# Attention outputs of a decoder trunk: two matmuls with high and low values side by side in place of three, and one PSUM bank for each key head

## Chip, core and metric

The kernel runs on one core of one Trainium2 chip. The metric is the device time of one execution in microseconds (us); lower is better. Five engines run side by side: TensorE (PE, matmuls; PEld are its weight loads), VectorE (DVE), ScalarE (ACT), GpSimd (POOL), and SyncE (SP), which here issues the DMAs. Each engine takes its instructions strictly in the order in which the program lists them.

## The reference

Two layers, each of five blocks on a residual stream of 256 tokens by 1024 features: a gated feed-forward block, a mixer, a second feed-forward block and a per-layer input. The mixer has two branches. The change is in branch B, attention with a window of 128 keys, 16 query heads and 4 key heads (four query heads share a key head), 64 features per head:

```python
u = rmsnorm(h, mix_norm); z = u @ w_in
# B: 128-query blocks; each sees its own and the block before
scores = einsum("bnqhgd,bnkhd->bnhgqk", qb, kw) * 64 ** -0.5
pr = exp(where(valid, scores, -inf) - mx)
attn = pr / (sum(pr) + exp(sink - mx))
out = einsum("bnhgqk,bnkhd->bnqhgd", attn, vw)          # the attention outputs
merged = sigmoid(g_m) * (hm @ w_branch_m) + sigmoid(g_a) * (out @ w_branch_a)
h = h + merged @ w_out
```

Branch A is a recurrent one (mLSTM) with a short causal convolution on its queries and keys. Weights and activations are fp32.

## The kernel before, in words

Every fp32 matrix is kept as two fp32r tiles, a high part (ScalarE casts it) and a low part (VectorE subtracts the high part from the source); `splitting` at L464 does this. A product takes three matmuls, high by high, high by low and low by high (`mm3`, L386). The first name behind the arrow in a row is the moving operand of the matmul, the second the stationary one; for weights `wh` and `wl` are the two parts.

Weights stream from HBM in 1 MB pieces (tile `raw`) and are split into `wh` and `wl`; a ring of eight pairs feeds the matmuls. All matmul outputs go into one pool of eight PSUM banks, 128 by 512 fp32 each (`bank`, L246). A tile takes a bank that another has given back, and its first matmul then waits for the last reader of the tile that had the bank before.

The order of the work on PE, ACT, DVE and SP is written by the kernel itself. Jobs (the matmuls of a projection) run one after the other. Chains, which are generators such as `scores` and `outputs` below, are advanced one step at each `tick` (L196), as soon as a planner (`Clock`, L60 to 111, with a cost per element for each engine) thinks that their last step is done. The planner knows engines and DMAs; it holds no banks. What it decides becomes the fixed order of each engine's queue; at run time only semaphores hold an engine.

The mixer's jobs in order, with the tile names that the rows carry: `kvq` (keys, values, queries), `v` (mLSTM values), `gt` (gate), `if` (mLSTM gates), `z` twice (convolution inputs), `ya` (the attention outputs times `w_branch_a`, L790 to 798), `og`, `z`, `gt`, `ym`, `yo`. The attention chains run beside `kvq` to `ya`. For a block of queries t, a pair of key heads p and a key head g in it, `outputs` (L1220) scales the probabilities `pr`, transposes them on PE into a bank `tp`, splits that into `ptd`, and multiplies by the values. A key head has 64 features, so the values stand in `vpad` with zeros in the other 64 columns of the stationary tile: two key heads add into the two halves of one bank `ha`, three matmuls of 512 columns for each block s of keys. When both heads are in, `ha` is split into `haT`, which shares its tile with `qT` (rows show it as `qT<-ha`). Block t = 0 has one block of keys, t = 1 has two.

Other tiles in the rows: `wif` are the weights of the mLSTM gates, split by two small ACT and two small DVE instructions; `cv`, `cy`, `qk` belong to the convolution (`conv`, L991), whose VectorE steps read the bank `z`; `wt` and `w` are mLSTM decay weights; `xn` and `uT` the normalized residual stream and its transpose. L130 is the line that issues every recorded instruction, so rows are told apart by tiles.

Of the kernel before, what the change touches and what calls it, by code (L numbers as in the profile page):

```python
# [11 lines left out]
F32 = mybir.dt.float32  # L12
F32R = mybir.dt.float32r
BF16 = mybir.dt.bfloat16
AF = mybir.ActivationFunctionType
ALU = mybir.AluOpType
# [6 lines left out]
NT = T // P  # L23
# [3 lines left out]
NB = 512  # L27
# [3 lines left out]
AQ, AKV, AD = 16, 4, 64  # L31
# [18 lines left out]
class Part:  # L50


    def __init__(self, c0, k, n):
        self.c0, self.k, self.n = c0, k, n
        self.hi = self.lo = self.ready = None
        self.fresh = True
        self.rows = None


class Clock:  # L60
# [18 lines left out]
    def begin(self, **ready):  # L79
        outer = self.stage  # L80
        self.stage = {**(outer or {}), **ready}
        return outer
# [1012 lines left out]
class Swa:  # L1095

    def __init__(self, tr, l):
        self.tr, self.nc = tr, tr.nc  # L1100
        self.l = l
        self.haT = self.qT = tr.new_T("qT")
        self.vpad, self.inputs = {}, {}

    def prepare(self):
        tr, nc, a, l = self.tr, self.nc, self.tr.a, self.l
# [2 lines left out]

    def begin(self):  # L1110
        tr, nc = self.tr, self.nc
        for s in range(NT):
            v = tr.slot("vpad", F32R)[:, : 2 * NB].rearrange("p (x h d) -> p x h d", x=2, h=AKV)
            nc.gpsimd.memset(v.bitcast(F32), 0.0)
            for part in range(2):
                self.vpad[s, part] = v[:, part]
        self.kT = tr.slot("kT", F32R)[:, : 4 * T].rearrange("p (x b t) -> p x b t", x=2, b=2)
        self.nsink = tr.small.tile([P, AQ], F32, tag="nsink", bufs=2, name=tr.name("nsink"))
        nc.vector.tensor_scalar(self.nsink, self.sink, -1.0, None, op0=ALU.mult)
# [20 lines left out]
    def keys(self, t, ps):  # L1140
        tr, nc = self.tr, self.nc
        n = AKV * AD
        r = yield from self.rms(ps[:, :n], AKV)
        kn = tr.scr("kn")[:, :n]
        nc.vector.tensor_tensor(kn.rearrange("p (h d) -> p h d", d=AD), ps[:, :n].rearrange("p (h d) -> p h d", d=AD),
                                r[:, :, None].to_broadcast([P, AKV, AD]), op=ALU.mult)
        for g in range(2):
            v = ps[:, n:].rearrange("p (b g d) -> p b g d", g=2, d=AD)[:, :, g, :]
            o = [self.vpad[t, part].rearrange("p (b g) d -> p b g d", g=2)[:, :, g, g * AD : (g + 1) * AD]
                 for part in range(2)]  # L1150
            yield from tr.splitting(o[0], o[1], v)
        tok = slice(t * P, (t + 1) * P)
        yield
        yield from self.put(self.kT[:, 0, :, tok], self.kT[:, 1, :, tok], tr.transposes(kn, 2), tr.gk)
# [65 lines left out]
    def outputs(self, t, p, g, acc, hd, pr, mx, den):  # L1220

        tr, nc = self.tr, self.nc
        tok = slice(t * P, (t + 1) * P)
        es = tr.col("es", 4)
        nc.vector.tensor_tensor(es, mx, self.sink[:, hd], op=ALU.add)
        yield
        nc.scalar.activation(es, es, AF.Exp)
        yield
        nc.vector.tensor_tensor(den, den, es, op=ALU.add)
        nc.vector.reciprocal(den, den)  # L1230
        yield
        for j in range(4):
            nc.scalar.mul(pr[:, j, :], pr[:, j, :], den[:, j : j + 1])
        yield
        total = 2 * (t + 1)
        for s in range(t + 1):
            ps = tr.bank("tp")
            for j in range(4):
                nc.tensor.transpose(ps[:, j * P : (j + 1) * P], pr[:, j, s * P : (s + 1) * P], tr.ident)
            yield  # L1240
            ptd = tr.slot("ptd", F32R)[:, : 2 * NB].rearrange("p (x n) -> p x n", x=2)
            yield from tr.splitting(ptd[:, 0], ptd[:, 1], ps)
            yield
            if (t, p) not in acc:
                acc[t, p] = [tr.bank("ha"), 0]
            out, n = acc[t, p]
            acc[t, p][1] += 1
            tr.mm3(out, self.vpad[s, 0][:, 2 * p + g, :], self.vpad[s, 1][:, 2 * p + g, :], ptd[:, 0], ptd[:, 1],
                   n == 0, n == total - 1)
        if n == total - 1:  # L1250
            yield
            yield from tr.splitting(self.haT[0](4 * p, tok, 4), self.haT[1](4 * p, tok, 4),
                                    out.rearrange("p (j t) -> p j t", j=4))


@with_exitstack
# [25 lines left out]
```

## Time and profile before

| what | value |
|---|---|
| median of three runs | 1375.36 us (1374.87 to 1376.43) |
| the profiled execution | 1374.73 us, of which the span of instructions is 1372.9 us |
| PE busy, PEld busy | 99% and 90% of the span |
| DVE busy, ACT busy | 63% and 54% |
| mean granted TensorE clock | 1.000 |
| HBM read | 241.34 MB, 177 GB/s |

A busy share is the time in which an engine had at least one instruction in hand. Matmuls are pipelined: a row of one matmul lasts longer than the distance to the next matmul's start, so what a matmul costs is read from starts, not from durations. ACT and DVE overlap the end of an instruction with the start of the next in the same way by some 0.1 us. The three runs differ by 0.11%.

### The profile page before, as it was taken

The page shows a single profiled execution, that of the slowest core. Times are in us where ns is not written, and L with a number is a line of the kernel's source. Part 1 is how long each engine was busy: PE and PEld are TensorE (multiplying, and loading weights), DVE is VectorE, ACT ScalarE, POOL GpSimd, SP SyncE. Part 2 cuts the span into 40 slices and gives each one's busy share as a digit, 9 for nine tenths or more (in the row PEclk, how much of TensorE's full clock was granted, in tenths as well). Part 3 has the DMA queues.
Part 4 walks back from the last instruction along what each step waited for, and adds up shares of the span by engine and source line. Part 5 has one row for each costly group of instructions (what it writes and reads, how often), then busy time and mean ns, then how long its engine had stood idle before and what let it go on. Part 6 is the DMA issues. An engine that isn't in the chain of part 4 may idle for free.

```text
span 1372.9 us, 21950 instructions
## 1 busy us (share of the span) xinstructions
PE 1359.6 (99%) x9016; PEld 1231.6 (90%) x9016; DVE 867.7 (63%) x1332; ACT 738.7 (54%) x1148; POOL 58.3 (4%) x84
## 2 busy tenths in 40 slices
PE   8999999999999999999999999999999999999998
PEld 6999888899899899988879998878998998999886
DVE  5655558777786665554665554586877876655544
ACT  5554345887565444443555443468875654544433
POOL 0000012000000000000000000120000000000000
PEclk9999999999999999999999999999999999999999
DMA  6665646254645465565456566454546554755651
GB/s 207 223 209 174 224 131 215 95 168 114 224 155 196 156 216 189 167 234 184 162 161 215 171 200 215 149 165 140 144 113 228 185 179 155 227 186 175 210 182 62
DMA packets 125831, 243.82 MB, mean 178 GB/s; under 512 B 14977, under 2 KB 23841, under 8 KB 125730
## 3 DMA queue, kind: packets, MB, share of 16 engines
q1 hardware_dynamic: 125730, 242.41, 55.1%
q8 instruction: 71, 1.16, 0.3%
q14 instruction: 30, 0.25, 0.1%
HBM read 241.34 MB, written 1.05 MB: 177 GB/s over the span
## 4 chain that ended last, share of the span: by engine, by line
PE 91%; DMA 3%; DVE 3%; ACT 1%; issue 0%; POOL 0%; SPq 0%; ACTq 0%; POOLq 0%
PE dn L130 17%; PE pg L130 16%; PE pu L130 14%; PE gt L130 7%; PE z L130 7%; PE gu L130 6%; PE v L130 3%; PE ya L130 3%; PE ym L130 3%; PE og L130 3%; PE yo L130 3%; PE kvq L130 3%; PE tp L130 2%; DVE wl L130 1%; DMA raw<-in_ffn_w_gate_dram 1%; DMA raw<-in_w_in_dram 1%
## 5 line engine op out<-in xcount | busy, mean ns | idle before, releaser
L130 DVE TENSOR_TENSOR wl<-raw,wh 128x1024 fp32r<-128x1024 f32 (+1 forms) x448 | 539.7, 1222 | 338.8 <-ACT wh L130 338.0
L130 ACT CAST wh<-raw 128x1024 fp32r<-128x1024 f32 x448 | 459.8, 1049 | 392.1 <-PE dn L130 78.6
L130 PE MATMUL dn<-wh,hid 128*128 128x512 f32 x688 | 218.1, 395 | 0.0
L130 PE MATMUL pg<-uT,wh 128*128 128x256 f32 x1088 | 194.6, 281 | 0.0
L130 PE MATMUL pu<-uT,wh 128*128 128x256 f32 x1088 | 193.7, 280 | 0.0
L130 PEld LDWEIGHTS pg<-uT,wh 128*128 128x128 f32 x1088 | 166.9, 188 | 0.2
L130 PEld LDWEIGHTS pu<-uT,wh 128*128 128x128 f32 x1088 | 166.9, 188 | 0.0
L130 PEld LDWEIGHTS dn<-wh,hid 128*128 128x128 f32 x688 | 129.2, 188 | 30.0
L130 PE MATMUL pu<-uT,wl 128*128 128x256 f32 x544 | 153.1, 281 | 0.0
L130 PE MATMUL pg<-uT,wl 128*128 128x256 f32 x544 | 153.0, 281 | 0.0
L130 PE MATMUL dn<-wl,hid 128*128 128x512 f32 x352 | 138.8, 394 | 0.0
L130 PEld LDWEIGHTS pg<-uT,wl 128*128 128x128 f32 x544 | 102.5, 188 | 0.0
L130 PEld LDWEIGHTS pu<-uT,wl 128*128 128x128 f32 x544 | 102.4, 188 | 0.0
L130 PE MATMUL z<-uT,wh 128*128 128x256 f32 x512 | 93.0, 283 | 0.0
L130 PE MATMUL gt<-uT,wh 128*128 128x256 f32 x512 | 92.2, 282 | 0.0
L130 PE MATMUL gu<-wh,uT 128*128 128x512 f32 x256 | 84.1, 405 | 1.5 <-ACT uT L130 1.5
L130 PEld LDWEIGHTS dn<-wl,hid 128*128 128x128 f32 x352 | 66.2, 188 | 15.2
L130 PEld LDWEIGHTS gt<-uT,wh 128*128 128x128 f32 x512 | 78.9, 188 | 0.8
L130 PEld LDWEIGHTS z<-uT,wh 128*128 128x128 f32 x512 | 78.7, 188 | 0.4
L130 PE MATMUL z<-uT,wl 128*128 128x256 f32 x256 | 71.9, 281 | 0.0
L130 PE MATMUL gt<-uT,wl 128*128 128x256 f32 x256 | 71.9, 281 | 0.0
L130 PE MATMUL kvq<-wh,uT 128*128 128x512 f32 x192 | 63.7, 401 | 0.0
(192 smaller groups left out, 2040.8 us busy)
## 6 DMA issues: line engine op xcount, KB each, us to landing
raw<-in_w_in_dram SPq DMA_DIRECT2D x60, 1024.0 KB, 5.1
raw<-in_ffn_w_up_dram SPq DMA_DIRECT2D x40, 1024.0 KB, 5.1
raw<-in_ffn_w_down_dram SPq DMA_DIRECT2D x40, 1024.0 KB, 5.2
raw<-in_ffn_w_gate_dram SPq DMA_DIRECT2D x39, 1024.0 KB, 5.2
raw<-in_w_branch_a_dram SPq DMA_DIRECT2D x16, 512.0 KB, 6.0
raw<-in_w_branch_m_dram SPq DMA_DIRECT2D x8, 1024.0 KB, 6.4
raw<-in_w_out_dram SPq DMA_DIRECT2D x8, 1024.0 KB, 5.2
raw<-in_ple_gate_w_dram SPq DMA_DIRECT2D x8, 1024.0 KB, 6.9
```

Of the source, the lines that this page charges most:

```text
L130: return issue(*args, **kw)
```

## The change

The values of a key head are no longer padded. Their high and low parts stand side by side in the 128 columns of one stationary tile `vv`, the high part in the half where the head's outputs belong (columns 0 to 63 for g = 0, 64 to 127 for g = 1), the low part in the other. Two matmuls for each block of keys, with the high and the low part of `ptd` as moving operand, fill a bank of the head's own: one half holds the products with the high values, the other those with the low values. ScalarE copies the low half out of the bank into a scratch tile `hc` (64 partitions by 512), VectorE adds it to the high half. The first head's bank of a pair collects the result of both; the second head's VectorE instruction writes its sum into the other half of that bank. Then it is split as before. The two zeroing instructions on GpSimd for `vpad` are gone.

```diff
     def begin(self):
-        for s in range(NT):
-            v = tr.slot("vpad", F32R)[:, : 2 * NB].rearrange("p (x h d) -> p x h d", x=2, h=AKV)
-            nc.gpsimd.memset(v.bitcast(F32), 0.0)
-            for part in range(2):
-                self.vpad[s, part] = v[:, part]
+        v = tr.slot("vv", F32R)[:, : 2 * NB].rearrange("p (s h d) -> p s h d", s=NT, h=AKV)
+        self.vv = [v[:, s] for s in range(NT)]
...
-            o = [self.vpad[t, part].rearrange("p (b g) d -> p b g d", g=2)[:, :, g, g * AD : (g + 1) * AD]
-                 for part in range(2)]
+            o = [self.vv[t].rearrange("p (b g) d -> p b g d", g=2)[:, :, g, r * AD : (r + 1) * AD] for r in (g, 1 - g)]
...
-        total = 2 * (t + 1)
         for s in range(t + 1):
...
-            if (t, p) not in acc:
-                acc[t, p] = [tr.bank("ha"), 0]
-            out, n = acc[t, p]
-            acc[t, p][1] += 1
-            tr.mm3(out, self.vpad[s, 0][:, 2 * p + g, :], self.vpad[s, 1][:, 2 * p + g, :], ptd[:, 0], ptd[:, 1],
-                   n == 0, n == total - 1)
-        if n == total - 1:
+            if s == 0:
+                out = tr.bank("ha")
+            for x in range(2):
+                nc.tensor.matmul(out, self.vv[s][:, 2 * p + g, :], ptd[:, x], start=s + x == 0, stop=s == t and x == 1)
+        yield
+        rows = [slice(r * AD, (r + 1) * AD) for r in (g, 1 - g)]
+        rest = tr.scr("hc")[rows[0]]
+        nc.scalar.copy(rest, out[rows[1]])
+        yield
+        first = (t, p) not in acc
+        both = acc.setdefault((t, p), out)
+        nc.vector.tensor_tensor(both[rows[0]], out[rows[0]], rest, op=ALU.add)
+        if not first:
             yield
             yield from tr.splitting(self.haT[0](4 * p, tok, 4), self.haT[1](4 * p, tok, 4),
-                                    out.rearrange("p (j t) -> p j t", j=4))
+                                    both.rearrange("p (j t) -> p j t", j=4))
```

The planner sees other costs, so the queues change in the mixers of both layers, in the same way in each.

VectorE in layer 1, where the attention outputs of block t = 0, heads p = 0, come up, before:

```order
L130 TENSOR_TENSOR ptd_2585<-tp_2574,ptd_2585 128x512 [waits Activation_49]
L130 TENSOR_TENSOR ptd_2599<-tp_2587,ptd_2599 128x512 [waits Activation_49]
L130 TENSOR_TENSOR wl_2631<-raw_2464,wh_2630 128x1024 [waits Activation_49]
L130 TENSOR_TENSOR v_2510<-v_2535,v_2507 128x2x256 [waits Activation_49]
L130 TENSOR_TENSOR wif_2704<-wif_1576,wif_2704 128x8x4 [waits Activation_49] x2
```

and at the same place now:

```order
L130 TENSOR_TENSOR ptd_2596<-tp_2584,ptd_2596 128x512 [waits Activation_49]
L130 TENSOR_TENSOR wif_2660<-wif_1576,wif_2660 128x8x4 [waits Activation_49] x2
L130 TENSOR_TENSOR wl_2628<-raw_2461,wh_2627 128x1024
L130 TENSOR_TENSOR v_2507<-v_2532,v_2504 128x2x256 [waits PE_49]
L130 TENSOR_TENSOR ha_2633<-ha_2633,hc_2645 64x512 [waits PE_49]
L130 TENSOR_TENSOR ha_2633<-ha_2647,hc_2670 64x512 [waits DVE_49,Activation_49]
```

The two `wif` instructions stand ahead of a weight split and a value split instead of behind them, and the two additions come last. On PE the scores of the next block, two banks `sc` side by side, waited for nothing of VectorE before; in the built program now the first of them takes the bank of `v_2532` and the second that of `ha_2647`:

```order
L130 MATMUL sc_2663<-kT_1994,qT_135 128x128 [waits PE_49]
L130 MATMUL sc_2664<-kT_1994,qT_135 128x128 [waits PE_49]
L130 MATMUL sc_2663<-kT_1994,qT_135 128x128
L130 MATMUL sc_2664<-kT_1994,qT_135 128x128
L130 MATMUL sc_2663<-kT_1994,qT_137 128x128
```

and the same two banks now:

```order
L130 MATMUL sc_2707<-kT_1991,qT_135 128x128 [waits DVE_49]
L130 MATMUL sc_2708<-kT_1991,qT_135 128x128 [waits DVE_49]
L130 MATMUL sc_2707<-kT_1991,qT_135 128x128
L130 MATMUL sc_2708<-kT_1991,qT_135 128x128
L130 MATMUL sc_2707<-kT_1991,qT_137 128x128
```

The wait of each bank's first matmul moved from PE's own earlier work to VectorE. The second place is on VectorE at the start of `ya`, where the convolution reads the banks `z_3301` and `z_3302`. Now:

```order
L130 TENSOR_TENSOR qk_3472<-cy_3451,qk_3472 128x512 [waits Activation_49]
L130 SCALAR_TENSOR_TENSOR cv_3485<-z_3301,feat_1988,cv_3485 128x255 [waits Activation_49]
L130 SCALAR_TENSOR_TENSOR cv_3485<-z_3301,feat_1988,cv_3485 128x254 [waits DVE_49]
L130 SCALAR_TENSOR_TENSOR cv_3485<-z_3301,feat_1988,cv_3485 128x253 [waits DVE_49]
L130 SCALAR_TENSOR_TENSOR cv_3488<-z_3302,feat_1988,cv_3488 128x255 [waits Activation_49]
L130 SCALAR_TENSOR_TENSOR cv_3488<-z_3302,feat_1988,cv_3488 128x254 [waits DVE_49]
L130 SCALAR_TENSOR_TENSOR cv_3488<-z_3302,feat_1988,cv_3488 128x253 [waits DVE_49]
L130 TENSOR_TENSOR ha_3386<-ha_3386,hc_3508 64x512 [waits Activation_49]
L130 SCALAR_TENSOR_TENSOR cv_3485<-z_3301,feat_1988,cv_3485 128x255
L130 SCALAR_TENSOR_TENSOR cv_3485<-z_3301,feat_1988,cv_3485 128x254 [waits DVE_49]
L130 SCALAR_TENSOR_TENSOR cv_3485<-z_3301,feat_1988,cv_3485 128x253 [waits DVE_49]
L130 TENSOR_TENSOR ha_3386<-ha_3432,hc_3552 64x512 [waits Activation_49]
```

Before, no `ha` instruction and no `ptd` stood among these; the `ptd` and the `qT<-ha` of the last attention group were ahead of them. `ya` uses four banks; the fourth, `ya_3494`, now takes the bank of `z_3301`, whose last reader is the ninth `cv` row above.

## Rows read from the trace of the kernel before

**Rows 1.** The page: busy us (share of the span) xinstructions of each engine.

```profile
PE 1359.6 (99%) x9016; PEld 1231.6 (90%) x9016; DVE 867.7 (63%) x1332; ACT 738.7 (54%) x1148; POOL 58.3 (4%) x84
```

**Rows 2.** Who PE waited for: us in total, times, longest; first and last of four.

```profile
PE tp L130 <- DVE xn L130: 3.5, 2, 2.1
...
PE gu L130 <- DVE wl L130: 0.8, 1, 0.8
```

**Rows 3.** The stretch with `kvq`, `v` and `gt` of layer 1: busy us, clock, DMA.

```profile
195.00:310.00 115.00, 114.93 (x739) 99.67 (x738) 85.49 (x208) 84.29 (x189) 13.37 (x19) 1.00 0.47 145
```

**Rows 4.** The chain that ended last, in order of time: start, us, what.

```profile
327.46 9.89 PE ya L130 x84
```

**Rows 5.** Groups of instructions by line and shape: busy us, mean ns | idle before.

```profile
L130 DVE TENSOR_TENSOR wl<-raw,wh 128x1024 fp32r<-128x1024 f32 x444 | 534.8, 1222 | 332.6 <-ACT wh L130 331.8 <-ACT mp L130 0.3
...
L130 PE MATMUL ha<-ptd,vpad 128*128 128x512 f32 x72 | 19.5, 397 | 0.0
...
L130 ACT CAST ptd<-tp 128x512 fp32r<-128x512 f32 x24 | 13.4, 586 | 12.7 <-PE tp L130 9.0 <-issue 3.6
...
L130 DVE SCALAR_TENSOR_TENSOR mg<-gate,ym 128x512 f32<-128x512 f32 x8 | 5.4, 681 | 0.0
...
L130 DVE TENSOR_TENSOR wl<-raw,wh 64x1024 fp32r<-64x1024 f32 x4 | 4.9, 1218 | 6.3 <-ACT wh L130 6.3
```

**Rows 6.** PE in order of time at the first `ha` group: start, us, what.

```profile
261.14 1.55 PE L130 MATMUL ha<-ptd,vpad 128*128 128x512 f32 x6
262.53 1.03 PE L130 MATMUL tp<-ident,pr 128*128 128x128 f32 x8
263.32 0.48 PE L130 MATMUL v<-wh,uT 128*128 128x512 f32 x1
263.64 0.39 PE L130 MATMUL v<-wl,uT 128*128 128x512 f32 x1
```

**Rows 7.** ACT in order of time at the same place.

```profile
262.77 0.59 ACT L130 CAST v<-v 128x512 fp32r<-128x512 f32 x1
263.24 0.60 ACT L130 CAST qT<-ha 128x512 fp32r<-128x512 f32 x1
263.72 1.08 ACT L130 CAST ptd<-tp 128x512 fp32r<-128x512 f32 x2
264.67 1.08 ACT L130 CAST wh<-raw 128x1024 fp32r<-128x1024 f32 x1
265.62 0.37 ACT L130 CAST wif<-wif 128x32 fp32r<-128x32 f32 x2
```

**Rows 8.** DVE in order of time at the same place.

```profile
264.06 0.68 DVE L130 TENSOR_TENSOR v<-v,v 128x512 fp32r<-128x512 f32 x1
265.90 0.31 DVE L130 TENSOR_TENSOR wif<-wif,wif 128x32 fp32r<-128x32 f32 x2 [1.16 <-ACT wif L130]
```

**Rows 9.** ACT in order of time ahead of `ya`.

```profile
320.24 1.28 ACT L130 ACT_TABLE_LOAD   x1
321.54 0.63 ACT L130 ACTIVATE cy<-cv 128x512 f32<-128x512 f32 x1
322.07 1.99 ACT L130 CAST wh<-raw 128x1024 fp32r<-128x1024 f32 x2
323.96 0.61 ACT L130 CAST qk<-cy 128x512 fp32r<-128x512 f32 x1
```

**Rows 10.** DVE in order of time in `ya`.

```profile
330.53 0.62 DVE L130 TENSOR_TENSOR wt<-wt,mask_st 128x128 f32<-128x128 f32 x2
332.68 0.69 DVE L130 TENSOR_TENSOR qk<-cy,qk 128x512 fp32r<-128x512 f32 x1 [1.53 <-ACT qk L130]
333.29 1.51 DVE L130 SCALAR_TENSOR_TENSOR cv<-z,feat,cv 128x255 f32<-128x255 f32 x3
334.72 1.22 DVE L130 TENSOR_TENSOR wl<-raw,wh 128x1024 fp32r<-128x1024 f32 x1
335.85 1.51 DVE L130 SCALAR_TENSOR_TENSOR cv<-z,feat,cv 128x255 f32<-128x255 f32 x3
```

More of the change, by code (lines that the diff above doesn't have):

```diff
@@ L1102, in __init__ @@
         self.haT = self.qT = tr.new_T("qT")
-        self.vpad, self.inputs = {}, {}
+        self.inputs = {}
     def prepare(self):
```

## The prediction

> **What bounds the kernel now.** First the busy shares: PE has work in hand for 99% of the span, VectorE for 63%, ScalarE for 54% [rows 1]. That share alone proves little, since a matmul's row is longer than its distance to the next, so I went on to the waits of PE: the largest and the smallest of four groups are 3.5 and 0.8 us, and their tiles (`xn`, `gu`) belong to norms and feed-forward blocks, none to the attention, `z` or `ya` of a mixer [rows 2]. Then the stretches: in the one with the first attention work of layer 1 PE is busy 114.93 of 115.00 us at a granted clock of 1.00, VectorE 85.49, ScalarE 84.29 [rows 3]. Last the order of time, which gives what a matmul costs from starts: six `ha` matmuls of 512 columns take 261.14 to 262.53, 0.232 us each [rows 6]; 84 `ya` matmuls of 256 columns take 9.89 us, 0.118 each [rows 4]. So a matmul left out in the mixer is worth its whole distance, and a wait put into PE's queue there costs its whole length: no later work of PE can give it back.
>
> **The change part by part, against the profiled execution (1374.73 us; its span is 1372.9, and 1.8 lie around it; it stands 0.6 below the median of the runs shown).**
>
> *Removed from PE.* Of 72 `ha` matmuls [rows 5] 48 are left, 24 fewer, at 0.232: **5.6 us gained**, half in each layer. Nothing hides this gain, since PE has no other limit there. The weight loads go with them and stand beside the matmuls.
>
> *Removed from GpSimd.* Four zeroing instructions between jobs. Nobody on PE waits for GpSimd in a mixer [rows 2]: nothing either way.
>
> *Added.* 16 ScalarE copies and 16 VectorE additions of 64 by 512. The trace has no such shape. Half the partitions do not halve the time: a subtraction of 64 by 1024 takes 1.218 us, one of 128 by 1024 1.222 [rows 5]. So I take the rows with as many elements per partition: 0.586 us for a 512-column ScalarE cast out of PSUM and 0.681 for a 512-column VectorE instruction with a PSUM and an SBUF operand [rows 5]; start to start 0.48 [rows 7] and 0.61 [rows 10]. Were it by partitions after all, half of that is the lower end. Per layer this is 8 × 0.48 = 3.8 us on ScalarE and 8 × 0.61 = 4.9 on VectorE, in a stretch where they are idle for 31 and 30 of 115 us [rows 3]. As a load that is hidden. Its price is decided by PE's waits, so I walked the three places where the new order gives PE a tight wait, each engine's instructions one behind the other at the distances of the rows.
>
> *Place 1: the scores behind the first attention outputs.* Until 261.14 both programs are alike. PE now does two `ha` (0.46), four transposes (0.40, half of 262.53 to 263.32), three `v` (0.32 behind transposes, then 0.23 twice: 0.78) [rows 6], the same three once more for the second head, and 18 `gt` at 0.118 (2.12): it reaches the two `sc` banks at 261.14 + 5.40 = 266.54. ScalarE: the `v` cast starts at 262.77 as before, the copy at 263.24 where `qT<-ha` stood, the `ptd` cast at 263.72, and the `wif` pair at 264.20 [rows 7]. VectorE had idled 1.16 us until `wif` came and was done with it at 266.21, 0.59 after ScalarE's start of the pair at 265.62 [rows 7, 8]. Now that pair stands ahead of a weight split, a `v` split and both additions. So: `wif` leaves VectorE free at 264.20 + 0.59 - 0.07 = 264.72; the weight split takes it to 265.85 (1.13 from 334.72 to 335.85 [rows 10]); the `v` split to 266.46, done at about 266.55: the first `sc` bank comes just in time. The first addition goes to 267.07, the second needs its end and is done at 267.85. PE wants that bank at 266.6 and gets it at 267.9: **a wait of 1.3 us**. Behind it in PE's queue stand all later matmuls, so it counts in full. With additions of half the time it would be 0.6; with the weight split alone ahead a little more, 1.4.
>
> *Place 2: the fourth bank of `ya`.* It was read last by the convolution's VectorE steps on the first `z` bank. I start both walks at the end of the transposes for the second `ptd` of the last attention group. PE from there: 42 `z` and 54 `ya` at 0.118 (11.3), six `ha` (1.4), four transposes (0.4), two `wt` and five tiny transposes, for which I take 0.6 to 0.8: 13.8. ScalarE: `ptd` 0.48, a table load 1.30, `cy` 0.53, two `wh` 1.89, `ptd` 0.48, `cy` 0.53, `qk` 0.61 until it is done: 5.8 [rows 7, 9]. Then VectorE: `qk` 0.61, two weight splits 2.26, `ptd` 0.61, two `wt` 0.55, `qk` 0.61, three `cv` 1.43, three `cv` 1.43, an addition 0.61, three `cv` 1.51 until done [rows 10]: 9.6. Together 15.4 against 13.8: **a wait of 1.6 us**. Without the addition and the two `ptd` splits in that queue, which stood earlier before, it would be nothing; the table load is in both programs.
>
> *Place 3: the low half of the last attention outputs, still in `ya`.* Once place 2 has let PE go, VectorE does an addition 0.61, two `wt` 0.55, three `cv` 1.43, two weight splits 2.26 and the split into `qT` 0.69, 5.5 us. PE has 43 matmuls of 0.118 before it needs that half, 5.1: **a wait of 0.4 us**. Before, this split was done ahead of the job.
>
> The Trainium skill (Perfetto Trace Analysis, section Optimizing Tensor Performance, Matmuls) says that independent matmul groups should rotate through different PSUM banks, so that emptying one overlaps the next group's matmuls. By it alone a bank for each head is a help and the sum would be the bare 5.6 us of gain. The same page (section Optimization Strategy) says that gaps which repeat on an engine that should be saturated can mean too little PSUM for the next tile, and by that the extra bank costs. In this trace no gap of that kind is seen, with PE at 114.93 of 115.00 us [rows 3]; the walk above decides without either.
>
> *Sum.* Waits 1.3 + 1.6 + 0.4 = 3.3 a layer, 6.6 in two; gain 5.6. Net 1.0 to 1.1 us more: 1374.73 + 1.1 = 1375.8 for the profiled run, and on the median of the runs shown **1376.5 us**, 0.08% above. Differences within 0.2% (2.75 us) are about what a measurement of this kernel can't tell from no change; I call that the same.
>
> **The rivals.**
>
> *A, the waits do not come, and PE gets its 5.6 us: 1369.8.* For it: VectorE and ScalarE are free for a quarter of the stretch [rows 3], and VectorE idled 1.16 us beside this very place [rows 8]; if `wif` is split earlier or the halved partitions halve the copies, place 1 shrinks to a few tenths, and a `qk` that comes 1.6 us earlier empties place 2. This is also what the skill's rule on rotating banks would give. Against it: an in-order queue puts the idle time behind `wif`, where it helps nobody. Partly so (place 2 alone gone) would be 1376.5 - 3.2 = 1373.3, still within 0.2%.
>
> *B, slower: a weight split waits at the two places.* The walks take it that each weight split's source is there when its turn comes. Weight splits that waited for ScalarE's cast are the largest entry of VectorE's idle time, 331.8 us over the span [rows 5]. If one split of 1.13 us stands late or twice in front of the banks at places 1 and 2, in both layers, this adds 4 × 1.13 = 4.5: 1381.0. It becomes slower by the bound above from 1.65 us more on, 0.4 at each of the four. Against it: weights are prefetched in a ring, and the one group of PE waits for a weight split is that of `gu`, outside the mixers [rows 2].
>
> *C, the change does not do what it says*: a two-pass group costs PE as much as three, because of the added hand-overs. Then the waits stand bare: 1376.5 + 5.6 = 1382. Against it: `ha` matmuls follow each other at 0.232 without any gap [rows 6], and weight loads fit in beside them.
>
> **How the numbers follow.** Forecast 0.57, A in full 0.14, B 0.25, C 0.04. The forecast's own range is 1373.3 (place 2 gone) to 1378.5 (each wait 0.3 longer, 6 × 0.3 = 1.8). For 8 in 10 I reach to A's end but for its last tenths and to most of B: 1370.2 to 1380.3. Faster by over 0.2% (below 1372.6): A and the forecast's low tail, 0.15. Slower (above 1378.1): B, C and a small tail, less the part of B that stays under 0.4 each, 0.27. The same: 0.58.
>
> **What would show it.** `ha` with 48 matmuls at 0.232; in the waits of PE new entries `sc` for VectorE's `ha` near 1.3 us, two times, and `ya` for VectorE's `cv` near 1.6 and its `qT` near 0.4, two each. The copies should take 0.58 to 0.59 us and the additions 0.68 to 0.69; half of these would prove the choice of rows wrong. If PE has no such waits and the time is near 1370, the walks are wrong; if there are waits in `gt` or `z` too, the order is tighter than I saw, and the time is nearer to B.

## Result, and the profile after

The changed kernel takes 1381.2 us (median of five runs, 1380.5 to 1385.6), the kernel before, run beside it, 1375.3. The ratio is 1.005, with a 95% interval from 1.0039 to 1.0061: slower by 5.9 us, and above the predicted range, which ended at 1380.3. The profiled execution took 1381.2 us with a span of 1379.4, against 1374.73 and 1372.9 before.

The page of the changed kernel, busy us (share of the span) and instructions of each engine, which answers to [rows 1]:

```profile
PE 1359.2 (99%) x8992; PEld 1230.6 (89%) x8992; DVE 876.3 (64%) x1348; ACT 747.4 (54%) x1164; POOL 51.9 (4%) x80
```

PE has 24 instructions fewer and the same busy time; VectorE and ScalarE have 16 more each. Nothing here tells where 6.5 us of span went. The instructions on the tile `ha` in the changed kernel (nanoseconds minimum/median/maximum, first and last start) show that the new work has the predicted size:

```profile
L130 PE MATMUL ha<-ptd,vv x48: 388/394/476, 260.2 to 1012.0; 128*128 128x512 f32 x48
L130 ACT COPY hc<-ha x16: 578/582/587, 262.4 to 1012.7; 64x512 f32<-64x512 f32 x16
L130 DVE TENSOR_TENSOR ha<-ha,hc x16: 679/700/710, 265.7 to 1017.1; 64x512 f32<-64x512 f32 x16
```

Whom PE waited for in the changed kernel (total us, times, longest), against [rows 2]:

```profile
PE tp L130 <- DVE xn L130: 4.3, 2, 2.7
PE ya L130 <- DVE cv L130: 3.9, 2, 2.2
...
PE sc L130 <- DVE ha L130: 2.2, 2, 1.1
PE ya L130 <- DVE qT L130: 0.7, 2, 0.4
PE tp L130 <- DVE sg L130: 0.6, 1, 0.6
...
PE sc L130 <- DVE v L130: 0.4, 2, 0.2
```

Three entries are the forecast's places, and there are three more things: a wait of `sc` for `v` at place 1, a norm hand-over (`tp<-xn`) that grew from 2.1 to 2.7 us, and one (`tp<-sg`) that was not there. The stretch of [rows 3] has PE busy 1.2 us less:

```profile
195.00:310.00 115.00, 113.70 (x740) 99.06 (x739) 88.61 (x216) 84.73 (x191) 11.30 (x16) 1.00 0.44 138
```

Place 1 in order of time, PE first (start, us, what, idle before it and who ended that), then VectorE:

```profile
265.37 0.28 PE L130 MATMUL gt<-uT,wl 128*128 128x256 f32 x1
265.86 0.33 PE L130 MATMUL sc<-kT,qT 64*128 64x128 f32 x1 [0.21 <-DVE v L130]
267.27 1.55 PE L130 MATMUL sc<-kT,qT 64*128 64x128 f32 x23 [1.09 <-DVE ha L130]
```

```profile
263.76 0.31 DVE L130 TENSOR_TENSOR wif<-wif,wif 128x32 fp32r<-128x32 f32 x2 [4.32 <-ACT wif L130]
263.99 1.22 DVE L130 TENSOR_TENSOR wl<-raw,wh 128x1024 fp32r<-128x1024 f32 x1
265.12 0.68 DVE L130 TENSOR_TENSOR v<-v,v 128x512 fp32r<-128x512 f32 x1
265.72 1.50 DVE L130 TENSOR_TENSOR ha<-ha,hc 64x512 f32<-64x512 f32 x2
```

ScalarE at the same place:

```profile
261.80 0.59 ACT L130 CAST v<-v 128x512 fp32r<-128x512 f32 x1
262.42 0.58 ACT L130 COPY hc<-ha 64x512 f32<-64x512 f32 x1
263.03 0.59 ACT L130 CAST ptd<-tp 128x512 fp32r<-128x512 f32 x1
263.51 0.34 ACT L130 CAST wif<-wif 128x32 fp32r<-128x32 f32 x2
```

VectorE is free of work for 4.32 us, but behind the `wif` pair, and then does everything in a row while PE stands. Counted from starts, PE's first `sc` comes 0.49 us after the `gt` matmul before it (0.12 is normal) and the second `sc` 1.41 after the first (0.06 normal): 0.37 + 1.35 = 1.7 us lost. The waits view shows less (0.21 + 1.09), because it counts idle time from the modelled end of a matmul and the loss runs from its start.

Places 2 and 3, PE and then VectorE:

```profile
331.78 0.28 PE L130 MATMUL ya<-qT,wl 128*128 128x256 f32 x1
334.27 0.50 PE L130 MATMUL ya<-qT,wh 128*128 128x256 f32 x2 [2.21 <-DVE cv L130]
...
339.32 0.28 PE L130 MATMUL ya<-qT,wh 128*128 128x256 f32 x1
339.96 0.39 PE L130 MATMUL ya<-qT,wh 128*128 128x256 f32 x1 [0.36 <-DVE qT L130]
```

```profile
329.27 2.93 DVE L130 SCALAR_TENSOR_TENSOR cv<-z,feat,cv 128x255 f32<-128x255 f32 x6
332.12 0.68 DVE L130 TENSOR_TENSOR ha<-ha,hc 64x512 f32<-64x512 f32 x1
332.72 1.50 DVE L130 SCALAR_TENSOR_TENSOR cv<-z,feat,cv 128x255 f32<-128x255 f32 x3
...
336.96 2.35 DVE L130 TENSOR_TENSOR wl<-raw,wh 128x1024 fp32r<-128x1024 f32 x2
339.22 0.68 DVE L130 TENSOR_TENSOR qT<-ha,qT 128x512 fp32r<-128x512 f32 x1
```

This is the predicted chain: the addition stands between the convolution's steps, the last of these frees the bank at 334.2, PE starts at 334.27; and the split into `qT`, behind two weight splits, lets it go on at 339.96. From starts that is 2.4 and 0.5 us in layer 1, 1.8 and 0.5 in layer 2.

Outside the mixers, at the norm between layer 1 and layer 2, the changed kernel in two-microsecond stretches (PE busy, weight loads, DVE, ACT, POOL, granted clock, DMA share, GB/s):

```profile
692.00:694.00 2.00, 1.30 (x9) 1.06 (x10) 1.30 (x2) 1.31 (x3) 0.00 (x0) 1.00 0.00 0
694.00:696.00 2.00, 2.00 (x8) 1.53 (x7) 1.36 (x2) 1.95 (x3) 0.00 (x0) 0.59 0.00 0
696.00:698.00 2.00, 2.00 (x7) 1.57 (x6) 0.91 (x2) 1.02 (x2) 0.00 (x0) 0.56 0.00 0
```

Here the granted clock fell to its lower level (1.2 GHz, shown as 0.50 where a stretch lies wholly in it) after PE had stood 2.7 us. The profiled run of the kernel before stood 2.1 us at this norm and kept 1.00.

To put the loss together I cut each trace at the first `kvq` and the last `yo` matmul of each layer, by their starts (us); "rest" ends at the start of the last matmul, and the 5.5 us behind it are the same in both kernels. The last column says whether the clock fell at the norm between the layers; the rows e1 to e4 are experiments that follow.

| trace | up to `kvq` | mixer 1 | between | mixer 2 | rest | clock fall |
|---|---|---|---|---|---|---|
| before | 198.69 | 276.05 | 403.05 | 275.91 | 213.69 | no |
| changed | 197.84 | 278.73 | 404.74 | 278.01 | 214.59 | yes |
| e1, two products, old order | 198.48 | 273.03 | 404.27 | 273.20 | 214.23 | yes |
| e2, gates early | 198.63 | 274.87 | 403.33 | 275.52 | 214.45 | no |
| e3, and sum in SBUF | 197.75 | 273.68 | 404.43 | 274.38 | 214.43 | yes |
| e4, before with gates early | 198.52 | 276.49 | 403.30 | 276.11 | 213.65 | yes |

From before to changed: -0.85 at the start, +2.68 and +2.10 in the mixers, +1.69 between, +0.90 in the rest; sum 6.52, the difference of the spans.

Outside the mixers every trace has the same matmuls in the same order (but for twelve in e7, e8 and e10), so the starts can be compared one by one. Of the +1.69 between, 0.69 has come up before the norm, spread thinly over matmuls that wait for nothing, and 0.57 is the longer wait at the norm. Behind it the lower clock costs 1.5 us, but 1.3 of that comes back within 30 us, 1.0 of it where the kernel before stands for weights (`gu` for `wl`, 0.8 in the waits view) and the changed kernel, being late, does not. The last 0.2 is spread thinly again. The +0.90 in the rest is nearly all one wait, `tp` for `sg`. The -0.85 at the start is this execution's luck: two more traces of the changed kernel (e5, e11) have 198.55 and 198.59 there.

### The profile page after: what moved, and what is told of

Same layout as the page of the kernel before. It is cut to its first block, busy times and chain, and to the rows that moved or that the text cites. A ratio compares the mean times of both kernels' runs of the same rounds, so it can differ in the third digit from the quotient of the medians.

```text
span 1379.4 us, 21920 instructions
## 1 busy us (share of the span) xinstructions
PE 1359.2 (99%) x8992; PEld 1230.6 (89%) x8992; DVE 876.3 (64%) x1348; ACT 747.4 (54%) x1164; POOL 51.9 (4%) x80
## 4 chain that ended last, share of the span: by engine, by line
PE 89%; DVE 5%; ACT 3%; DMA 2%; issue 1%; POOL 0%; SPq 0%; ACTq 0%; POOLq 0%
PE dn L130 17%; PE pg L130 16%; PE pu L130 14%; PE gt L130 6%; PE gu L130 6%; PE z L130 5%; PE kvq L130 5%; PE ym L130 3%; PE og L130 3%; PE yo L130 3%; PE v L130 2%; PE tp L130 2%; PE ya L130 2%; DVE wl L130 2%; DMA raw<-in_ffn_w_gate_dram 1%; ACT wh L130 1%
```

## Experiments

Each kernel was timed in turn with the kernel before on one chip; the ratio is to that. In the edits, names are those of the code shown above.

**e1, two of three products with the old order.** In the kernel before:

```diff
-            tr.mm3(out, self.vpad[s, 0][...], self.vpad[s, 1][...], ptd[:, 0], ptd[:, 1], n == 0, n == total - 1)
+            for x in range(2):
+                nc.tensor.matmul(out, self.vpad[s, 0][:, 2 * p + g, :], ptd[:, x], start=n + x == 0,
+                                 stop=n == total - 1 and x == 1)
+            tr.clock.charge("tensor", NB)
```

> The kernel before with only two of the three products of an attention output (low half of v times high half of the weights is left out); the planner is still charged for the third, so every queue keeps the order of before, with 24 matmuls fewer and no copies, additions or extra banks. Theory W (a pass is worth 0.232 us, and the changed kernel lost 8.6 us in its new waits): 1375.3 - 24 x 0.232 = 1369.7 us, waits of TensorE as in the kernel before. Rival C (two passes cost as much as three): 1375.3 us. Theory K (the half-clock stretch at the hand-over to layer 2 comes whatever the mixers do, as soon as the phase of the weights there moves): 1371 to 1372 us, with a stretch of granted clock near 0.6 there.

Measured: 1370.26 us beside 1374.52, ratio 0.9967 (0.9955 to 0.998). The two mixers became 3.02 and 2.71 us shorter, 5.73 together, where 24 matmuls at 0.232 make 5.57. A pass less is worth its whole distance. The time fell by less, 4.3 us, since "between" grew by 1.2; it lies between the two expectations. The clock fell at the norm here too (theory K), although nothing in this kernel waits in a mixer, and PE had stood 2.7 us there:

```profile
PE tp L130 <- DVE xn L130: 4.0, 2, 2.7
```

**e2, the gate weights split early.** In the changed kernel, one job moved (L749 and L783):

```diff
-        job(self.pair(w_in, C_V), xT, "v", rec.values)
+        job(self.pair(w_in, C_V), xT, "v", rec.values, rec.gate_weights)
...
-        self.jobs.append(rec.gate_weights)
```

> The changed kernel with one job moved: the split of the gate weights (wif) runs at the start of the v projection instead of after it, so that VectorE's queue does not stand behind it for 4.3 us when the first two additions come. Theory W with independent places: place 1 goes (0.38 + 1.36 and 0.33 + 1.36 = 3.4 us), places 2 and 3 stay: 1381.2 - 3.4 = 1377.8 us. Theory W with banks that move along (the last bank of ya now follows a transpose and not z, and another pair of scores follows an added ha bank): places 2 and 3 go too (2.9 and 2.3 us) and a wait sc<-ha of about 1.4 us comes once in each layer: 1381.2 - 8.6 + 2.8 = 1375.4 us with the half-clock stretch, 1373 without it. Rival (the loss is the 32 new instructions on VectorE and ScalarE as such, not where they wait): 1381 us.

Measured: 1374.65 us, ratio 1.0 (0.9991 to 1.0009). This is the case in which the banks move along: all entries of the three places are gone from PE's waits, and one new one came, smaller than I expected and for `qT`, not `ha`:

```profile
PE tp L130 <- DVE xn L130: 3.9, 2, 2.0
...
PE sc L130 <- DVE qT L130: 1.2, 2, 0.6
...
```

The mixers are 6.35 shorter than the changed kernel's. From starts the new wait costs 1.2 and 1.1 us (against e3, which has the same matmuls in the same order), and 8.6 less these is 6.3. The clock did not fall at the norm in this trace; for that case 1373 was expected, so the time is some 1.7 us above its expectation. The rival (16 copies and 16 additions cost something as such) is refuted as the cause: they are all still there. It is not shown which place gave what, since the move changed all three.

**e3, and the sum in a scratch tile.** e2 and:

```diff
-        both = acc.setdefault((t, p), out)
+        both = acc[t, p] if not first else acc.setdefault((t, p), tr.scr("hb"))
```

> As the run before it, and the sum of both halves is written to a scratch tile in SBUF instead of back to the first head's bank, so each ha bank is free after its own addition. Theory W: no bank of scores or ya then follows an addition or a convolution that is late; all 8.6 us of waits go: 1381.2 - 8.6 = 1372.6 us if the half-clock stretch at the hand-over stays (theory K), 1370 to 1371 us if it goes with them; faster than both kernels either way. Rival (the new instructions as such): 1380 us or more.

Measured: 1372.93 us, ratio 0.9985 (0.9976 to 0.9994). No wait of PE in a mixer is left; the list holds only norms, feed-forward weights and the start:

```profile
PE tp L130 <- DVE xn L130: 3.6, 2, 2.6
PE g L130 <- DVE pick L263: 2.4, 1, 2.4
PE gu L130 <- ACT uT L130: 0.9, 1, 0.9
PE gu L130 <- DVE wl L130: 0.9, 2, 0.7
PE tp L130 <- DVE sg L130: 0.4, 1, 0.4
```

Against the changed kernel the mixers are shorter by 5.05 and 3.63, 8.7 us, which is what the gaps at the three places add up to (1.7 + 2.4 + 0.5 and 1.7 + 1.8 + 0.5 = 8.6). So the waits are the loss in the mixers. But e3 does not reach e1, which has as many matmuls: its mixers are 0.65 and 1.18 longer without any wait (distances between matmuls; see the last section).

**e4, control.** The same move in the kernel before.

> Control: the kernel before with the same job moved and nothing else. Theory W: no wait of TensorE depends on it there: 1375.3 us, within 0.5. Rival (what the two runs before it gain is a gain of the move itself): 1371 to 1373 us.

Measured: 1375.39 us, ratio 1.0005 (0.9996 to 1.0014). The move alone gives nothing, so its gain in e2 and e3 is that of the removed waits.

**e5, the changed kernel once more.**

> The changed kernel once more, unaltered, for a second trace. If the waits are the program's own: sc<-ha 2.2 us in 2, ya<-cv 3.9 in 2, ya<-qT 0.7 in 2 again within 0.2, and a mixer of layer 1 of 278.7 us between its first kvq and its last yo matmul. If the hand-over to layer 2 is the run's chance, its wait (2.7 us) and the half-clock stretch of 3.4 us behind it need not come again.

Measured: 1387.24 us in a single run. The waits are the program's own: 2.2, 3.3 and 0.7 us at the three places, place 2 with 1.6 in each layer, as predicted, where the first trace had 2.2 in one of them; so the 3.9 expected of this run was too much. The wait at the norm (2.7 us) and the fall of the clock there for 3.4 us came again. New was the clock in the mixers: in both layers it fell right behind place 1. Layer 1, before, in and after that stretch (columns as above):

```profile
266.00:268.50 2.50, 1.26 (x16) 0.92 (x15) 2.36 (x5) 2.49 (x4) 0.00 (x0) 1.00 0.61 189
268.50:275.50 7.00, 7.00 (x40) 6.58 (x38) 6.26 (x24) 0.00 (x0) 0.00 (x0) 0.51 0.23 86
275.50:278.00 2.50, 2.50 (x22) 2.37 (x21) 1.39 (x4) 1.91 (x7) 0.00 (x0) 1.00 0.86 274
```

The mixers took 280.93 and 281.03 us, 2.2 and 3.0 more than in the first trace (2.9 and 3.0 more than in e11, a third trace of this program with the same 1.6 to 1.7 at place 2). So a wait that PE was given can cost more than its length, in some executions of one program and not in others. The Trainium skill (TensorE: Matmul & The Clock Gate, section A second HAM failure mode: psum-queue depth-cycling) tells of a kernel in which short idle stretches of PE, between groups of matmuls that cycle through PSUM banks, made the clock go up and down. This trace agrees in part: one fall in each mixer, to 0.51, behind a single wait for two banks, with no going up and down; the first trace of the same program, with the same wait and 1.00 behind it, shows that it need not come.

**e6, the norm made late in the kernel before.** One VectorE instruction more at the norm between the layers (the lines that count the norms are left out here and in e7):

```diff
             xn.append(self.scr("xn"))
+            if t == 0 and n == 0 and self.norms == 5:
+                self.tc.nc.vector.scalar_tensor_tensor(xn[n], self.h[t][:, half(n)], r, g[n], op0=ALU.mult, op1=ALU.mult)
```

> The kernel before with one VectorE instruction more (0.69 us): the first half of xn of the first tokens is computed twice at the hand-over from layer 1 to layer 2, nowhere else. Theory K (a longer wait of TensorE there brings a stretch at half clock behind it): wait tp<-xn 2.1 + 0.7 = 2.8 us, granted clock near 0.6 in the 4 us behind it, 0.7 + 1.5 us later, less up to 0.9 us that the next weights would have been waited for: 1374.5 + 1.3 = 1375.8 us. Rival (the stretch comes by chance or by the mixers): wait 2.8 us, clock 1.00 there, 1375.2 us or less.

Measured: 1375.81 us beside 1374.76, ratio 1.0007 (0.9998 to 1.0016): the expected time, but not told from no change. In its trace PE stood longer than expected (3.9 us, not 2.8), and the clock fell before it went on; that the time came out as expected is therefore partly luck. First PE's row, then the windows:

```profile
690.69 1.97 PE L130 MATMUL tp<-ident,xn 128*128 128x128 f32 x8 [3.91 <-DVE xn L130]
```

```profile
687.00:690.70 3.70, 0.01 (x1) 0.01 (x1) 3.02 (x6) 1.46 (x5) 0.55 (x1) 0.80 0.08 30
690.70:696.00 5.30, 5.30 (x17) 4.53 (x18) 2.03 (x4) 3.66 (x5) 0.00 (x0) 0.50 0.00 0
```

**e7 and e8, the wait filled.** Twelve matmuls of 384 columns with no use, at that norm alone, into the bank that the transposes then overwrite; e7 in the changed kernel, e8 in e3:

```diff
         ps = self.bank("tp")
+        for _ in range(self.warm):      # 12 at this norm, else 0
+            self.tc.nc.tensor.matmul(ps[:, : T + P], self.pick[:, :1].to_broadcast([P, P]), self.rows2, start=True, stop=True)
```

> The changed kernel with 12 idle matmuls of 384 columns (0.175 us each, 2.1 in all) in front of the transposes at that hand-over, into the bank that the transposes then overwrite; nothing else differs. Theory K: TensorE's idle stretch shrinks from 2.7 to some 0.6 us, the granted clock stays at 1.00, and the time falls by 0.6 to 1.5 us: 1379.7 to 1380.6. Rival (the fall has another cause): the stretch at half clock stays, 1381.2 us.

> The third run (gate weights early, sum in SBUF) with the same 12 matmuls at the hand-over. Theory K: 1372.9 - 0.6 to 1.5 = 1371.4 to 1372.3 us with clock 1.00 behind the hand-over; rival: 1372.9 us.

Measured: e7 1379.93 us, ratio 1.0036 (1.0024 to 1.0049); e8 1371.89, ratio 0.9978 (0.997 to 0.9987). The clock stayed up behind the norm in both traces. e7, the stretch with the wait and the one behind it:

```profile
689.00:693.00 4.00, 3.20 (x19) 2.61 (x19) 2.87 (x5) 1.86 (x6) 0.55 (x1) 1.00 0.28 107
693.00:697.00 4.00, 4.00 (x21) 3.29 (x20) 1.90 (x3) 3.35 (x5) 0.00 (x0) 1.00 0.00 0
```

So the lower clock there goes with a standing PE, seen from both sides: it came when the wait was made longer and stayed away when the wait was filled, in one trace of each kernel. What it costs is not settled: both medians moved as expected (1.0 to 1.3 us), but the intervals overlap those without the filling. In the traces "between" went from 404.43 to 403.60 in e8, but in e7 it stayed at 404.86, since PE now waited 0.8 us for the feed-forward weights, as in the kernel before. So in these traces the gain of e7 does not come from the stretch behind the norm: its trace is shorter in mixer 1 (277.78, with 1.6 at place 2) and in the rest. e8 is faster than both kernels, by 2.9 us against the kernel before on its chip.

**e9, only the sum in a scratch tile.**

> The changed kernel with only the second of the two edits of the third run: the sum goes to a scratch tile in SBUF, the gate weights stay where they are. Theory Q (VectorE's queue is what is late, the bank only decides which matmul meets it): place 1 keeps about half of its 1.7 us a layer, the wait for cv in ya shrinks but the one for the low half of qT grows from 0.4 by what the other lost, since that split stands at the same place of VectorE's queue: together 1 to 2 us less, 1379.5 us. Rival (the banks decide): all three places go, 1373 us.

Measured: 1380.27 us, ratio 1.0046 (1.0034 to 1.0059). Theory Q holds: at places 2 and 3 the wait for the bank is gone and the same time comes back as a wait for the data, 1.9 us in each layer (from starts 2.1 and 1.6 less at place 2, 1.5 more at place 3 in each). Place 1 lost 0.9 and 0.8 of its 1.7 us, about half, as expected:

```profile
PE ya L130 <- DVE qT L130: 3.8, 2, 1.9
...
PE sc L130 <- ACT wh L130: 0.7, 2, 0.4
```

VectorE's queue in that trace is the one of the changed kernel, `qT` last:

```profile
336.67 2.35 DVE L130 TENSOR_TENSOR wl<-raw,wh 128x1024 fp32r<-128x1024 f32 x2
338.94 0.69 DVE L130 TENSOR_TENSOR qT<-hb,qT 128x512 fp32r<-128x512 f32 x1
```

Here the clock fell behind the wait for `qT` in both layers, which cost 1.5 us in each (from starts, against the first trace of the changed kernel); without that the mixers would be 1.6 and 0.8 shorter than there.

**e10, control for the filling.** The kernel before with the same twelve matmuls.

> Control for the bridged runs: the kernel before with the same 12 matmuls at the hand-over. Its wait there is 2.1 us and its profiled run had no half-clock stretch, though the mean clocks of its timed runs lie between 0.998 and 1.000. Theory K: at most the runs with a stretch become shorter, 1374.0 us (0 to 0.8 us less than before); a gain of 1 us or more would mean that the bridge helps for another reason than the clock.

Measured: 1374.73 us beside 1374.6, ratio 0.9999 (0.9991 to 1.0008). No gain of its own. PE's row in its trace shows a wait of 0.40 us left and the clock stayed at 1.00.

**e11, the changed kernel timed again.**

> The changed kernel again, timed, on the chip of the two runs above: 5.9 us over the kernel before (1.0043 of it). The spread of its runs shows how often a stretch at half clock comes behind the new waits of the mixers (about 2.2 to 3.0 us each, as in the run whose trace had them in both layers).

Measured: 1381.59 us, ratio 1.0056 (1.0042 to 1.007). The result stands. Mixers 278.01 and 277.98, again with 1.6 to 1.7 at place 2; at the norm PE stood 3.2 us and the clock fell. The clock did not fall in its mixers. Of the eleven runs of the changed kernel, 1387.2, 1385.6 and 1384.7 us have the lowest mean clocks (0.994, 0.996 and 0.997; the others 0.998 or 0.999), so falls inside the mixers, as in e5, may have come in two runs more; without a trace this is not shown.

## Why the prediction was wrong

It said 1376.5; 1381.2 came, a step of +6.5 in the profiled runs where +1.1 was predicted.

*Removed from PE: right.* 5.6 predicted, 5.73 in e1. *Added work: right in size and in being hidden.* The copies took 0.58 us, the additions 0.70 (0.68 predicted); half the partitions did not halve them. In e3 they cost no wait.

*Place 1: right in mechanism, too small.* 1.3 predicted, 1.7 measured. The walk let the first `sc` bank come "just in time". But it had put the copy at 0.48 us from start to start like a cast; in the rows of ScalarE above there is 0.62 ahead of it and 0.61 behind it. So `wif` came 0.3 us late on ScalarE (263.51; the walk, moved by the 0.98 us that this trace runs ahead there, has 263.22), and with it `v` and both additions on VectorE, while PE was there when I had said (265.49 against 265.56).

*Place 2: right in mechanism, size nearly so.* 1.6 predicted; the waits view gives 1.6 to 1.7 in both layers of e5 and e11 and in layer 2 of the first trace, 2.2 in its layer 1; the loss from starts is 0.2 more each (1.8 and 2.4). *Place 3: right*, 0.4 in the view, 0.5 from starts. Together 8.6 us of waits from starts where the sum had 6.6.

*The step that failed is the sum.* It took the three places for the only terms and put everything else at nothing without giving a reason: that matmuls keep their distance when the order of the queues changes, and that the stretches outside the mixers stay as they were. Of the 5.4 us that are missing, the three waits account for 2.0. Larger distances between matmuls that wait for nothing account for 2.7: 1.8 in the mixers (e3 against e1; the changed kernel's own mixers are 10.5 longer than e1's, 8.6 of it waits) and 0.9 between them. The norm between the layers gives 0.8, of which 0.6 is its longer wait and 0.2 what is left of the clock's fall; the wait of `tp` for `sg` and little else in layer 2's last blocks gives 0.9. The start gave 0.85 back, by luck, and the gain was 0.2 larger: 2.0 + 2.7 + 0.8 + 0.9 - 0.85 - 0.2 = 5.4. In e11, a later trace of the same program, that last wait is absent (+0.18 in the rest), the norm's wait is 3.2, and the distances are the same, so the distances and the three waits belong to the program. The norm's wait is a matter of phase. Ahead of it, one row of the kernel before and then the changed kernel's:

```profile
682.54 1.05 ACT L130 CAST wh<-raw 128x1024 fp32r<-128x1024 f32 x1 [1.29 <-DMA raw<-in_ffn_w_gate_dram]
```

```profile
685.65 1.05 ACT L130 CAST wh<-raw 128x1024 fp32r<-128x1024 f32 x1 [1.37 <-DMA raw<-in_ffn_w_gate_dram]
...
686.73 1.23 DVE L130 TENSOR_TENSOR wl<-raw,wh 128x1024 fp32r<-128x1024 f32 x1 [1.19 <-ACT wh L130]
...
687.87 0.69 DVE L130 SCALAR_TENSOR_TENSOR sg<-sg,pp 128x512 f32<-128x512 f32 x1
```

The residual's last update (`sg`) stands behind a weight split, that behind a cast, and that behind a DMA. The cast starts 3.99 us ahead of PE's last `pg` matmul (689.64), in the kernel before 4.58 ahead (682.54 and 687.12): 0.59 less, as much as the wait grew. e1 and e3 have the same instructions there and waits of 2.7 and 2.6; e2 has 2.0. Why a given shift of PE brings the weights earlier or later against it is open.

*Rivals.* A (no waits) is what e3 makes of the change, though at 1372.9 and not at 1369.8. B had the time, 1381.0, by coincidence: no weight split stood late at places 1 and 2; the loss there was the order I had walked. C is refuted by the changed kernel's own rows, hand-overs and all, where two `ha` matmuls take 0.47 us, 0.235 each; e1 adds that a pass less is worth its distance:

```profile
260.16 0.63 PE L130 MATMUL ha<-ptd,vv 128*128 128x512 f32 x2
260.63 0.60 PE L130 MATMUL tp<-ident,pr 128*128 128x128 f32 x4
```

The rule on rotating banks (the Trainium skill, Perfetto Trace Analysis, Optimizing Tensor Performance, Matmuls) did not carry here: more banks in use meant that a matmul met a bank whose reader was late, 2.2 and 3.9 us in the waits; its other sentence (Optimization Strategy), that repeated gaps can mean too little PSUM, fits the waits for banks at places 1 and 2, but e9, which frees the banks early, keeps the time at places 2 and 3, where VectorE's queue is what is late.

## What to carry to other kernels

A pass taken from a saturated engine gives its distance back (5.73 us here, 5.57 by the rows), but the work that replaces it is paid where an in-order queue puts it: look up what stands ahead of the new instruction on its engine, and which bank the next matmul inherits; moving one small job here was worth some 6.5 us. When a wait for a bank goes, look for the wait for data that stands behind it on the same engine. Count a new wait from start to start, and treat a time within 0.2% as open even with every wait sized: the distances between matmuls alone differ by some 2.7 us between these two programs, also where both have the same matmuls in the same order. What a fall of the clock costs depends on what PE would have waited for behind it.

## What the runs showed of the hardware that I had not expected

The clock at the norm between the layers: PE stood 2.04 (e2) and 2.08 us (before) with 1.00 behind it, and 2.11 (e9), 2.42 (e4), 2.57 (e3), 2.66 (changed), 2.69 (e1), 2.70 (e5), 3.23 (e11) and 3.91 us (e6) with a fall to the lower level for 3.4 us, in e6 for 6.8. The length of the wait alone does not decide: in e9 the clock fell behind waits of 1.9 us in the mixers, and in e5 for 6.8 us behind place 1, where PE stood 0.2 and 1.1 us and two other traces of the same program kept 1.00. The timed runs of the kernel before have mean clocks from 0.996 to 1.000, so it too falls in some of them, at a place that these runs do not tell.

The distance between matmuls depends on the program, also where nothing waits (means of the starts of neighbours in one tile, those within a tenth of the normal distance). In layer 1's `ym`, the same matmuls of 256 columns start 115.4 ns apart in the kernel before, e1, e6 and e10, which share one order, and 118.1 to 118.3 in all other traces, among them e4, which differs from the kernel before by one moved job alone; in layer 2 it is 117.9 to 118.4 in all. `gt` in layer 2 has 117.5 to 117.6 in the kernel before, e1, e4, e6 and e10, 118.2 to 118.6 in the changed kernel and all that come from it. Traces of one program agree within 0.5 ns. Multiplied by their counts, such differences between e3 and e1 come to 0.7 us in mixer 1 (0.5 of it in `ym`) and 1.0 in mixer 2, where e3 is 0.65 and 1.18 longer. Between the mixers, where all programs have the same matmuls in the same order, all five traces with the changed kernel's order (changed, e5, e7, e9, e11) are 0.7 us behind the kernel before when they reach the norm, and e1, e6 and e10 are level with it. What in the programs causes it was not tried.
